# Queries and keys of a hybrid attention layer: the rotated columns of eight heads gathered into one projection unit, the plain ones into three, with the order of tasks laid out anew

## The chip, the cores and the metric

One core of one Trainium2 chip runs one launch of the whole layer. The metric is the device time of that launch in microseconds (us). The engines are TensorE (PE: matmuls; PEld: its weight loads), VectorE (DVE), ScalarE (ACT), GpSimd (POOL), and SyncE (SP), on which this kernel issues its DMAs. Each engine works through its own queue strictly in order.

## The reference, cut to what matters

The layer has 512 positions and a model width of 1024. One projection gives the queries, keys and values of two token mixers, an indexer's queries and keys, and branch gates:

```python
proj = x @ w_in            # qa ka va (12 heads), qb kb vb (12 heads), qi (8), ki (1), wi, gates
qa, ka, qi, ki, qb, kb = partial_rope(...)   # heads of 64 columns

def partial_rope(x, cos, sin):               # r = 8
    x1, x2, rest = x[..., :r], x[..., r:2 * r], x[..., 2 * r:]
    return concatenate([x1 * cos - x2 * sin, x2 * cos + x1 * sin, rest], axis=-1)
```

So of a head's 64 columns only the first 16 are rotated; the 48 others pass unchanged. Mixer A scores each query against the keys that an indexer picks (the 128 highest of up to 512, by `top_k`), mixer B attends in three dilated windows (groups of 4 heads with strides 1, 4 and 16) whose outputs are combined by their softmax denominators. Two gated branch products, an output projection, layer norm, a SwiGLU network and a second layer norm follow. All is in float32; each product is made of three matmuls on split operands (high x high, high x low, low x high).

## The kernel before, in words

**Units.** The columns of `w_in` come in units of 128 columns x 1024 rows (a `raw` tile of 128 x 1024). SP loads a unit, ACT copies its high part (`whi`, L347), DVE or POOL subtracts for the low part (`wlo`, L362), and `project()` makes 24 matmuls of 512 columns (L415 to L417) into one PSUM tile with the 128 columns of two heads on its partitions. Two such PSUM tiles exist (tag `pj`).

**Rotation.** Of the 28 units with queries and keys (28 head pairs), each goes through `rope()`: DVE shuffles the PSUM tile's partitions (L495), DVE multiplies it by a cosine table (L496), POOL multiplies the shuffled copy by a sine table (L497), and DVE adds the two (L499, or L502, which also regroups the positions by their remainder of four). The tables hold 1 and 0 for the 48 plain columns, so a full tile of 128 partitions is rotated though 32 of them change. Then `parts()` splits the result: ACT copies the high part (L508), DVE subtracts for the low part (L362).

**Stacks.** PE's scores want stacks: tiles of 128 partitions that hold a head's high part on 64 partitions and its high or low part on the other 64. `move()` assembles them by DMAs from SBUF to SBUF of 64 partitions each; SP issues 144 of them (all DMAs go through L331).

**Top-k.** `topk_steps()` finds the 128 highest of each row by 16 rounds of DVE's `MAX8` (L684) and `MATCH_REPLACE8` (L685) for each of three blocks of queries (256, 384 and 512 keys). Its rounds take turns on DVE with whatever else is queued there. Between them DVE also makes mixer B's masked scores (L768), the factors that combine its groups (L802 to L811), its output sums (L870 to L879) and the rotations.

**Order.** A string `ORDER` lists tasks: K index keys, I index heads, k/q/r/s and a/b units of mixers B and A, v the strided values, B0 to B3 mixer B's scores, X the exchange of its statistics over DRAM, M0 to M3 its mixing, W value chunks, H0 to H5 mixer A's head pairs, G gate units, T four top-k rounds. A planner (`Plan.order`) runs the listed tasks through a model of the engines with a price for each instruction, the free slots of each pool, and turns between DVE and POOL for operations marked `shared`, and emits each engine's queue in the order that it finds. The price of a DMA is `0.06 + nbytes / 361e3` us there.

Of the kernel before, what the change touches and what calls it, by code (L numbers as in the profile page):

```python
# [51 lines left out]
ORDER = ("G12 k0 r1 q0 G14 K G0 I1 r0 v I0 s0 b1 I3 G5 I2 G13 s1 r3 T s3 T a1 G2 B1 r2 k1 T q1 B0 B3 s2 B2 T T W0 T "  # L52
         "a4 X M2 G9 W1 a0 H1 b0 T M1 G7 T a3 M3 b5 M0 W2 T b2 a5 H0 b3 G8 H3 b4 G4 H5 a2 G11 G3 H2 H4 T T G1 G15 T "
         "G6 G10").split()

H = (slice(0, 64), slice(64, 128))
SWAP = list(range(8, 16)) + list(range(8)) + list(range(16, 32))
# [233 lines left out]
def layer(ctx, tc, xT, xN, pos, wp, bg, ln, cst, out):  # L291
# [38 lines left out]
    def dma(dst, dst_ap, src_ap, nbytes, reads=(), key=None, prio=None):  # L330
        P.op("SP", 0.06 + nbytes / 361e3, lambda e: nc.sync.dma_start(dst_ap(), src_ap()),  # L331
             reads, [(dst, key)], lag=DMA_LAG, prio=prio)
# [4 lines left out]
    def load_unit(lo_eng, pieces=1):  # L337

        u = unit[0]
        unit[0] += 1  # L340
        raw, hi, lo = P.buf("raw", FT, (128, 1024)), P.buf("whi", FR, (128, 1024)), P.buf("wlo", FR, (128, 1024))
        n = 1024 // pieces

        def piece(i):
            c = slice(i * n, (i + 1) * n)
            dma(raw, lambda: raw[:, c], lambda: wp[u * 128:(u + 1) * 128, c], 512 * n, key=i)
            P.op("ACT", ac(n, 1), lambda e: A.activation(hi[:, c], raw[:, c], AF.Copy), [(raw, i)], [(hi, i)])  # L347
            sub(lo_eng, n, lambda: lo[:, c], lambda: raw[:, c], lambda: hi[:, c].bitcast(FT),
                [(raw, i), (hi, i)], [(lo, i)])
# [55 lines left out]
    def next_unit(lo_eng):  # L405
        return first_units.pop(0) if first_units else load_unit(lo_eng)

    def project(w, tag="pj", t0=0):

        hi, lo, pieces, _ = w  # L410
        p = P.buf(tag)
        for ko in range(KO):
            def f(e, ko=ko):
                c = slice(ko * 128, (ko + 1) * 128)
                nc.tensor.matmul(p[:, t0:], hi[:, c], xhi[ko][:, t0:], start=ko == 0, stop=False)  # L415
                nc.tensor.matmul(p[:, t0:], hi[:, c], xlo[ko][:, t0:], start=False, stop=False)  # L416
                nc.tensor.matmul(p[:, t0:], lo[:, c], xhi[ko][:, t0:], start=False, stop=ko == KO - 1)  # L417
            k = ko * pieces // KO
            P.op("PE", 3 * mm(S - t0), f, [(hi, k), (lo, k), xhi[ko], xlo[ko]], [p])
        return p  # L420


    def rope_tables():
        n = NB * 8
        r_ = [fixed(f"rope{i}", (128, n)) for i in range(8)]
        pf, ang, c, d, hi, lo, u, r = r_
        prod = P.buf("rp", FT, (128, 2 * N_PIECE, n))
        rnd = P.buf("rp", FT, (128, 2 * N_PIECE, n))

        def v(cost, fn, reads, writes):  # L430
            P.op("DVE", cost, lambda e: fn(), reads, writes, prio=20)
# [31 lines left out]
        sn, cn = P.buf("rp", FT, (128, NB, 2, 8)), P.buf("rp", FT, (128, NB, 8))  # L463
        P.op("ACT", 0.15, lambda e: A.activation(sn[:, :, 1, :], a3(u), AF.Sin, scale=TWO_PI), [u], [(sn, 1)])
        P.op("ACT", 0.15, lambda e: A.activation(cn.tile, a3(r), AF.Sin, scale=TWO_PI), [r], [cn])
        v(small, lambda: V.tensor_scalar(sn[:, :, 0, :], sn[:, :, 1, :], -1.0, None, ALU.mult), [(sn, 1)], [(sn, 0)])
        for h in (0, 64):
            v(dv(64), lambda h=h: V.tensor_copy(wide_s[:, :, h:h + 16], sn.tile.rearrange("p b a f -> p b (a f)")),
              [sn], [(wide_s, h)])
            v(dv(64), lambda h=h: V.tensor_copy(wide_c[:, :, h:h + 16].rearrange("p b (a f) -> p b a f", a=2),  # L470
                                                bc(cn[:, :, None, :], [128, NB, 2, 8])), [cn], [(wide_c, h)])
# [14 lines left out]
    sn_rows, cn_rows = (lambda: sn[:, :, 1, :]), (lambda: cn.tile)  # L486
# [5 lines left out]
    def rope(p, regroup=False, t0=0):  # L492
# [4 lines left out]
        P.op("POOL", po(n), lambda e: G.tensor_tensor(t[:, t0:], t[:, t0:], TS[:, t0:], ALU.mult), [t, TS], [t])  # L497
# [8 lines left out]
    def parts(r, lo_tag, hi_tag="rt", t0=0):  # L506
        hi, lo = P.buf(hi_tag, FR), P.buf(lo_tag, FR)
# [4 lines left out]
    def move(dst, d, src, s, t0=0):  # L512
        dma(dst, lambda: dst[H[d], t0:].bitcast(FT), lambda: src[H[s], t0:].bitcast(FT), 256 * (S - t0), [src], d)

    def q_stacks(r, t0=0):

        hi, lo = parts(r, "rt", t0=t0)
        o = []
        for e in range(2):
            s = P.buf("qk", FR)  # L520
            move(s, e, hi, e, t0)
            move(s, 1 - e, lo, e, t0)
            o.append(s)
        return o

    def k_stacks(r):

        o = []
        for part in parts(r, "rt"):
            for e in range(2):  # L530
                s = P.buf("qk", FR)
                for x in range(2):
                    move(s, x, part, e)
                o.append(s)
        return [(o[0], o[2]), (o[1], o[3])]

    def k_blocks(r):

        o = []
        for part in parts(r, "rt"):  # L540
            for x in range(2):
                t = P.buf("qk", FR)
                P.op("POOL", 0.46, lambda e, t=t: G.memset(t.tile.bitcast(FT), 0.0), [], [t])
                for e in range(2):
                    dma(t, lambda t=t, e=e: t.tile.bitcast(FT).rearrange("p (r e m) -> p r e m", r=2, e=2)[H[e], :, e],
                        lambda part=part, x=x, e=e: part.tile.bitcast(FT).rearrange("p (r m) -> p r m", r=4)[
                            H[e], 2 * x:2 * x + 2], 65536, [part], e)
                o.append(t)
        return o[:2], o[2:]
# [113 lines left out]
    def index_heads(pr):  # L663

        qs = q_stacks(rope(project(next_unit("POOL"), t0=128), t0=128), t0=128)
# [13 lines left out]
    def topk_steps():  # L679
        for b in range(1, NB):  # L680
            n = (b + 1) * 128
            for _ in range(TOPK // 8):
                m = P.buf("z", FT, (128, 8))
                P.op("DVE", dv(n), lambda e, m=m, b=b: V.max(m.tile, acc[b].tile), [acc[b]], [m])  # L684
                P.op("DVE", dv(n), lambda e, m=m, b=b: V.match_replace(acc[b].tile, m.tile, acc[b].tile, TAKEN),  # L685
                     [acc[b], m], [acc[b]])
                yield
            P.op("DVE", dv2(n), lambda e, b=b: V.tensor_scalar(acc[b].tile, acc[b].tile, -2.0e38, NEG,
                                                               ALU.is_gt, ALU.mult), [acc[b]], [acc[b]])
# [104 lines left out]
    def b_factors(own, other, name):  # L794
# [6 lines left out]
        v = lambda fn, r, w: P.op("DVE", c, lambda e: fn(), r, w)  # L801
# [28 lines left out]
    def b_mix(i, dst):  # L830
# [48 lines left out]
        P.op("DVE", dv(512), lambda e: V.tensor_add(dst[d], x1[d], x2[d]), [x1, x2], [(dst, odd)])  # L879
# [57 lines left out]
    def q_pair(name):  # L937
        store[name] = q_stacks(rope(project(next_unit("POOL"))))

    def k_pair(name):  # L940
        store[name] = k_stacks(rope(project(next_unit("POOL"))))

# [3 lines left out]
        "q": lambda i: q_pair(f"q{i}"),  # L946
        "k": lambda i: k_pair(f"k{i}"),
        "r": lambda i: store.update({f"r{i}": parts(rope(project(next_unit("POOL")), True), "qk", "qk")}),
        "s": lambda i: store.update({f"s{i}": k_blocks(rope(project(next_unit("POOL")), True))}),
        "v": strided_values,  # L950
        "B": lambda i: b_logits(i, store[f"q{i // 2}"][i % 2], store[f"k{i // 2}"][i % 2],
                                store[f"r{i}"], store[f"s{i}"]),
# [3 lines left out]
        "a": lambda i: q_pair(f"a{i}"),  # L956
        "b": lambda i: k_pair(f"b{i}"),
        "H": lambda n: a_pair(n, store[f"VA{n // 2}"], store[f"a{n}"], store[f"b{n}"], out_tile(n)),
# [233 lines left out]
def _pack(np, inputs):  # L1192
# [76 lines left out]
```

## Time and profile before

| | |
|---|---|
| runs shown | 886.59, 888.36, 888.82 us (median 888.36) |
| profiled execution | 886.41 us, its span 884.6 us |
| busy share of PE, DVE, ACT, POOL | 96%, 59%, 41%, 19% |
| mean granted TensorE clock | 0.990 |

The span runs from the first to the last instruction; 1.8 us of the profiled execution lie around it. A busy PE is not PE at its peak: where the granted clock is below 1, the same matmuls take longer. The projections, both mixers and the top-k fill about the first 430 us; branch products, output projection and feed-forward network follow.

### The profile page before, as it was taken

What the parts mean: (1) busy time and instruction counts of PE and PEld (TensorE: products, weight loads), DVE (VectorE), ACT (ScalarE), POOL (GpSimd) and SP (SyncE); (2) the same over time, 40 slices, a digit from 0 to 9 for tenths busy, and PEclk for the clock granted to TensorE, in tenths of its full rate; (3) what the DMA queues carried; (4) which work ended last, traced back from release to release, by engine and by line L of the source; (5) the groups of instructions that cost most, each with busy time, mean ns of one, the idle gap of its engine ahead of it and who ended that gap; (6) DMA issues with size and microseconds to landing.
All of it is one profiled execution on the core that took longest, in us unless ns stands there. A gap on an engine that the chain in (4) does not pass through costs nothing.

```text
span 884.6 us, 11508 instructions
## 1 busy us (share of the span) xinstructions
PE 853.0 (96%) x4183; PEld 723.9 (82%) x4183; DVE 519.1 (59%) x1132; ACT 361.3 (41%) x769; POOL 167.8 (19%) x115
## 2 busy tenths in 40 slices
PE   8999999988889999999999999999999999999996
PEld 5888988878778888888888898888888888888885
DVE  7636467998996866868576853333333333222357
ACT  5333344345477546969644132222222222221210
POOL 3634544743332342320000100000000000000001
PEclk9999999999999999999999999999999999999999
DMA  6623362444415345321436303232233222222321
GB/s 206 190 96 114 114 183 71 129 130 121 122 49 143 90 141 151 97 96 48 156 113 231 120 16 104 95 98 97 101 101 103 98 96 95 96 96 96 119 72 72
DMA packets 41321, 98.69 MB, mean 112 GB/s; under 512 B 6960, under 2 KB 13360, under 8 KB 41264
## 3 DMA queue, kind: packets, MB, share of 16 engines
q1 hardware_dynamic: 41264, 97.95, 35.4%
q8 instruction: 33, 0.54, 0.3%
q14 instruction: 24, 0.20, 0.1%
HBM read 79.55 MB, written 2.13 MB: 92 GB/s over the span
## 4 chain that ended last, share of the span: by engine, by line
PE 75%; DVE 14%; DMA 3%; issue 2%; ACT 2%; SPq 2%; POOL 1%; DVEq 0%; POOLq 0%; ACTq 0%
PE ps L1092 9%; PE ps L1093 9%; PE ps L1094 9%; PE ps L1121 5%; PE ps L1119 5%; PE ps L1120 5%; PE ps L415 4%; PE ps L416 4%; PE ps L417 4%; PE ps L566 2%; DVE s L685 2%; DVE z L684 2%; PE ps L722 2%; PE ps L1059 2%; PE ps L1060 2%
## 5 line engine op out<-in xcount | busy, mean ns | idle before, releaser
L347 ACT ACTIVATE whi<-raw 128x1024 fp32r<-128x1024 f32 (+2 forms) x133 | 134.4, 1013 | 205.9 <-issue 83.4
L362 DVE TENSOR_TENSOR wlo<-raw,whi 128x1024 fp32r<-128x1024 f32 (+1 forms) x83 | 98.5, 1187 | 165.3 <-ACT whi L347 165.3
L362 POOL TENSOR_TENSOR wlo<-raw,whi 128x1024 fp32r<-128x1024 f32 (+2 forms) x50 | 115.3, 2310 | 152.7 <-ACT whi L347 139.2
L415 PE MATMUL ps<-s,whi 128*128 128x512 f32 (+1 forms) x352 | 141.2, 401 | 0.5 <-ACT s L391 0.5
L1092 PE MATMUL ps<-s,whi 128*128 128x512 f32 (+1 forms) x368 | 139.8, 380 | 0.0
L1093 PE MATMUL ps<-s,whi 128*128 128x512 f32 (+1 forms) x368 | 139.8, 380 | 0.0
L1094 PE MATMUL ps<-s,wlo 128*128 128x512 f32 (+1 forms) x368 | 139.8, 380 | 0.0
L416 PE MATMUL ps<-s,whi 128*128 128x512 f32 (+1 forms) x352 | 137.6, 391 | 1.8 <-DVE s L362 1.7
L417 PE MATMUL ps<-s,wlo 128*128 128x512 f32 (+1 forms) x352 | 136.8, 389 | 0.0
L1032 POOL TENSOR_TENSOR z<-z,nhalf 128x1 f32<-128x1 f32 x8 | 7.6, 955 | 479.3 <-DVE z L1031 479.3
L1094 PEld LDWEIGHTS ps<-s,wlo 128*128 128x128 f32 x368 | 69.2, 188 | 13.2
L1092 PEld LDWEIGHTS ps<-s,whi 128*128 128x128 f32 x368 | 69.2, 188 | 13.2
L1093 PEld LDWEIGHTS ps<-s,whi 128*128 128x128 f32 x368 | 69.2, 188 | 12.9
L416 PEld LDWEIGHTS ps<-s,whi 128*128 128x128 f32 x352 | 67.2, 191 | 13.8 <-DVE s L362 4.1
L417 PEld LDWEIGHTS ps<-s,wlo 128*128 128x128 f32 x352 | 66.8, 190 | 13.1
L415 PEld LDWEIGHTS ps<-s,whi 128*128 128x128 f32 x352 | 67.2, 191 | 11.7 <-ACT s L391 1.6
L362 DVE TENSOR_TENSOR s<-s,s 128x512 fp32r<-128x512 f32 (+1 forms) x74 | 52.7, 714 | 7.6 <-ACT s L508 4.2
L1119 PE MATMUL ps<-whi,s 128*128 128x512 f32 x136 | 52.9, 389 | 0.0
L1120 PE MATMUL ps<-wlo,s 128*128 128x512 f32 x136 | 52.9, 389 | 0.0
L1121 PE MATMUL ps<-whi,s 128*128 128x512 f32 x136 | 52.9, 389 | 0.0
L497 POOL TENSOR_TENSOR s<-s,tab 128x512 f32<-128x512 f32 (+1 forms) x28 | 35.5, 1268 | 78.6 <-DVE s L495 62.7
L1106 ACT ACTIVATE s<-ps 128x512 f32<-128x512 f32 x22 | 13.2, 598 | 86.8 <-PE ps L1094 86.8
(167 smaller groups left out, 1531.2 us busy)
## 6 DMA issues: line engine op xcount, KB each, us to landing
raw<-in_wp SPq DMA_DIRECT2D x136, 512.0 KB, 3.2
s<-s SPq DMA_DIRECT2D x96, 128.0 KB, 2.3
s<-in_xT SPq DMA_DIRECT2D x8, 256.0 KB, 4.7
s<-s SPq DMA_DIRECT2D x32, 64.0 KB, 2.0
s<-in_ln SPq DMA_DIRECT2D x8, 256.0 KB, 4.7
s<-in_xN SPq DMA_DIRECT2D x8, 256.0 KB, 5.3
out<-s SPq DMA_DIRECT2D x7, 256.0 KB, 2.1
s<-s SPq DMA_DIRECT2D x16, 96.0 KB, 2.5
```

What stands on the lines that cost most here:

```text
L347: P.op("ACT", ac(n, 1), lambda e: A.activation(hi[:, c], raw[:, c], AF.Copy), [(raw, i)], [(hi, i)])
L362: P.op(eng, cost, lambda e: ENG[e].tensor_tensor(dst(), a(), b(), ALU.subtract), reads, writes, shared=True)
L415: nc.tensor.matmul(p[:, t0:], hi[:, c], xhi[ko][:, t0:], start=ko == 0, stop=False)
L416: nc.tensor.matmul(p[:, t0:], hi[:, c], xlo[ko][:, t0:], start=False, stop=False)
L417: nc.tensor.matmul(p[:, t0:], lo[:, c], xhi[ko][:, t0:], start=False, stop=ko == KO - 1)
L497: P.op("POOL", po(n), lambda e: G.tensor_tensor(t[:, t0:], t[:, t0:], TS[:, t0:], ALU.mult), [t, TS], [t])
L1092: nc.tensor.matmul(p[:, c], hi[:, k], x1hi[ko][:, c], start=ko == 0, stop=False)
L1093: nc.tensor.matmul(p[:, c], hi[:, k], x1lo[ko][:, c], start=False, stop=False)
L1094: nc.tensor.matmul(p[:, c], lo[:, k], x1hi[ko][:, c], start=False, stop=ko == KO - 1)
L1119: nc.tensor.matmul(sums[:, :cols], hs[k][0][:, t], hi(), start=k == first, stop=False)
L1120: nc.tensor.matmul(sums[:, :cols], hs[k][0][:, t], lo(), start=False, stop=False)
L1121: nc.tensor.matmul(sums[:, :cols], hs[k][1][:, t], hi(), start=False, stop=k == last)
```

## The change

The 28 units stay 28, but are cut otherwise. For each eight heads (seven groups: the indexer's, three of mixer A, three of mixer B) unit 0 holds the 8 x 16 rotated columns and units 1 to 3 hold the 8 x 48 plain ones. Only unit 0 is rotated (7 instead of 28), and its second multiplication is made by DVE, not POOL. The plain units are split straight from PSUM: ACT copies the high part, DVE subtracts. A head now lies in two or three tiles, so its stacks are put together from pieces of 16, 32 or 48 rows, and SP issues 348 such DMAs instead of 144. POOL's low parts of the weights are made in halves of 512 columns, of which the first can be used earlier; the tables are made by one broadcast copy each; the planner's price of a DMA is at least 0.44, some more DVE operations are marked `shared`, and two top-k prices are a little higher. `ORDER` is new.

```diff
-ORDER = ("G12 k0 r1 q0 G14 K G0 I1 r0 v I0 s0 b1 I3 G5 I2 G13 s1 r3 T s3 T a1 G2 B1 r2 k1 T q1 B0 B3 s2 B2 T T W0 T "
+ORDER = ("G10 i0 G12 G6 i1 d0 i2 e0 W0 d1 i3 K G7 G13 e1 I1 e2 e4 I2 e3 I0 d2 a8 I3 B1 G15 T T T e5 B0 G2 e6 a0 d3 "
...
-        P.op("POOL", po(n), lambda e: G.tensor_tensor(t[:, t0:], t[:, t0:], TS[:, t0:], ALU.mult), [t, TS], [t])
+        P.op("DVE", dv(n), lambda e: V.tensor_mul(t[:, t0:], t[:, t0:], TS[:, t0:]), [t, TS], [t], shared=True)
...
+    def plain_parts(p, regroup, t0):
+        hi, lo = P.buf("rt", FR), P.buf("rt", FR)
+        to = (lambda t: reg(t.tile)) if regroup else lambda t: t[:, t0:]
+        src = (lambda: nat(p.tile)) if regroup else lambda: p[:, t0:]
+        P.op("ACT", ac(S - t0), lambda e: A.activation(to(hi), src(), AF.Copy), [p], [hi])
+        P.op("DVE", dv(S - t0), lambda e: V.tensor_tensor(to(lo), src(), to(hi).bitcast(FT), ALU.subtract),
+             [p, hi], [lo])
+        return hi, lo
...
+    def move(dst, d, src, s, n, t0=0):
+        dma(dst, lambda: dst[d:d + n, t0:].bitcast(FT), lambda: src[s:s + n, t0:].bitcast(FT), 4 * n * (S - t0),
+            [src], d)
...
+    def sides(name, j, puts, regroup=False, t0=0):
+
+        p = project(next_unit("POOL"), t0=t0)
+        if j == 0:
+            turned[name] = rotated_parts(p, regroup, t0)
+            return
+        parts = plain_parts(p, regroup, t0)
+        for s, put in enumerate(puts):
+            for unit_, row, n, first in plain_rows(s):
+                if unit_ == j - 1:
+                    if first == 0:
+                        put(turned[name], ROT * s, ROT, 0)
+                    put(parts, row, n, ROT + first)
...
-        "q": lambda i: q_pair(f"q{i}"),
-        "k": lambda i: k_pair(f"k{i}"),
...
+        "i": lambda j: sides("i", j, [put_q(f"i{h}", 128) for h in range(8)], t0=128),
+        "a": lambda n: sides(f"a{n // 4}", n % 4, qk_sides("a", n // 4 * 4)),
+        "d": lambda j: sides("d", j, qk_sides("d", 0)),
+        "e": lambda n: sides(f"e{n // 4}", n % 4, rs_sides(n // 4), True),
...
+    def side_unit(j, firsts):
+
+        rot = [w_in[:, c:c + ROT] for c in firsts]
+        rest = [w_in[:, c + ROT:c + 64] for c in firsts]
+        tile_unit(np.concatenate(rot, 1) if j == 0 else np.concatenate(rest, 1)[:, (j - 1) * 128:j * 128])
```

What this does to the queues shows best in three places. The first is DVE between two rounds of the first top-k block. Before, the sum of one rotation (L502) and the first rows of the next (L495 shuffle, L496 cosine) stand there (`s_121` is the block's scores):

```order
L502 TENSOR_TENSOR s_1525<-s_1476,s_1468 128x128x4
L495 STREAM_SHUFFLE s_1532<-ps_1456 128x512
L496 TENSOR_TENSOR s_1534<-ps_1456,tab_89 128x512
L685 MATCH_REPLACE s_121<-z_1518,s_121 128x256
L684 MAX z_1544<-s_121 128x8
L685 MATCH_REPLACE s_121<-z_1544,s_121 128x256
```

In the changed kernel the rows at that place are mostly plain splits (L536) and mixer B's scores (L834, before L768); the block's scores are `s_113`:

```order
L751 MATCH_REPLACE s_113<-z_1667,s_113 128x256
L750 MAX z_1690<-s_113 128x8
L834 ISA s_1703,z_91<-ps_1685,cs 128x128
L834 ISA z_91 128x1
L751 MATCH_REPLACE s_113<-z_1690,s_113 128x256
L536 TENSOR_TENSOR s_1712<-ps_1579,s_1692 128x128x4
L750 MAX z_1718<-s_113 128x8
L834 ISA s_1703,z_91<-ps_1694,cs 128x256
```

A unit that took three DVE rows before its split now takes none; between the first and the last `MAX` stand 246 DVE rows before and 220 after, with nine rotations before and two after.

The second place is SP's queue. Before, a unit's stacks are eight moves of 64 rows behind one weight load, here a unit of group s (`64x2x128`) behind the split of an index head:

```order
L331 DMA raw_1252<-in_wp 128x1024
L331 DMA raw_1292<-in_wp 128x1024
L331 DMA s_1327<-s_1319 64x384
L331 DMA s_1331<-s_1319 64x384
L331 DMA s_1327<-s_1325 64x384
L331 DMA s_1331<-s_1325 64x384
L331 DMA raw_1357<-in_wp 128x1024
L331 DMA s_1403<-s_1440 64x2x128 x2
L331 DMA s_1407<-s_1440 64x2x128 x2
```

In the changed kernel, before mixer B's first scores, moves of 16, 32 and 48 rows from the rotated tile (such as `s_531`) and a plain one (`s_1428`, `s_1437`) stand behind each other:

```order
L346 DMA raw_1430<-in_wp 128x1024
L346 DMA s_618<-s_1428 16x512
L346 DMA s_618<-s_1437 16x512
L346 DMA s_1411<-s_1428 48x512 x2
L346 DMA s_1421<-s_1437 48x512 x2
L346 DMA raw_1463<-in_wp 128x1024
L346 DMA s_1517<-s_531 16x512 x2
L346 DMA s_1527<-s_549 16x512 x2
L346 DMA s_1517<-s_1428 48x512 x2
L346 DMA s_1527<-s_1437 48x512 x2
L346 DMA s_1565<-s_531 16x512
```

Weight loads (`raw`) now stand behind more moves than before, and a stack is complete only when the last of its four to six pieces has landed.

The third place is PE's queue between mixer B's scores and its mixing, whose transposes are L722 (after: L788). Before, two units (L415 to L417, 48 rows) and 30 rows of a value chunk (L579 to L581) lie between the last scores (L558) and the first transpose, which these rows reach:

```order
L581 MATMUL ps_2325<-wlo_2294,s_277 128x256
L579 MATMUL ps_2378<-whi_2221,s_151 128x256
L580 MATMUL ps_2378<-whi_2221,s_160 128x256
L581 MATMUL ps_2378<-wlo_2237,s_151 128x256
L579 MATMUL ps_2378<-whi_2221,s_164 128x256
L580 MATMUL ps_2378<-whi_2221,s_175 128x256
L581 MATMUL ps_2378<-wlo_2237,s_164 128x256
L722 MATMUL ps_2390<-cs,s_2150 128x128
```

After, the strided values (`v`, L678 to L680, 96 rows of 512 columns) lie there; these are their end:

```order
L678 MATMUL ps_2312<-whi_2361,s_264 128x512
L679 MATMUL ps_2312<-whi_2361,s_271 128x512
L680 MATMUL ps_2312<-wlo_2372,s_264 128x512
L678 MATMUL ps_2320<-whi_2361,s_264 128x512
L679 MATMUL ps_2320<-whi_2361,s_271 128x512
L680 MATMUL ps_2320<-wlo_2372,s_264 128x512
L788 MATMUL ps_2533<-cs,s_2104 128x128
```

PE has 4030 such rows before and after, and from the last gate unit on its queue is the same. The `v` rows stood earlier in the queue before.

## Rows read from the trace of the kernel before

**Rows 1.** Busy time by stretch (a:b, length, PE, PEld, DVE, ACT, POOL, clock, DMA, GB/s).

```profile
0.00:50.00 50.00, 45.88 (x210) 37.03 (x211) 31.39 (x64) 22.02 (x39) 20.09 (x24) 1.00 0.61 186
50.00:143.70 93.70, 89.16 (x430) 80.88 (x429) 51.11 (x77) 36.17 (x61) 44.63 (x27) 1.00 0.42 126
143.70:260.10 116.40, 105.87 (x588) 92.77 (x587) 111.66 (x303) 59.67 (x148) 50.58 (x33) 0.96 0.37 108
260.10:380.00 119.90, 115.98 (x663) 99.43 (x662) 92.16 (x293) 79.78 (x229) 42.48 (x22) 0.99 0.42 115
380.00:500.00 120.00, 119.21 (x572) 99.29 (x571) 88.45 (x201) 70.05 (x166) 4.38 (x3) 1.00 0.42 140
...
800.00:885.00 85.00, 76.90 (x354) 64.11 (x352) 39.03 (x64) 13.08 (x17) 3.69 (x4) 0.97 0.26 88
```

**Rows 2.** What PE waited for: total us, times, longest.

```profile
PE ps L566 <- DMA s<-s: 4.6, 3, 3.2
PE ps L722 <- ACT s L827: 3.9, 1, 3.9
...
PE ps L558 <- DVE z L768: 2.9, 1, 2.9
```

**Rows 3.** Instructions of the top-k's MAX8: min/median/max ns, first and last start.

```profile
L684 DVE MAX8 z<-s x48: 401/556/698, 143.7 to 259.4; 128x8 f32<-128x256 f32 x16, 128x8 f32<-128x384 f32 x16, 128x8 f32<-128x512 f32 x16
```

**Rows 4.** DVE's groups by shape, 143.7 to 260.1 us.

```profile
L502 DVE TENSOR_TENSOR s<-s,s 128x512 f32<-128x512 f32 x5 | 8.2, 1646 | 0.0
...
L495 DVE STREAM_SHUFFLE s<-ps 128x512 f32<-128x512 f32 x9 | 6.8, 752 | 0.0
...
L496 DVE TENSOR_TENSOR s<-ps,tab 128x512 f32<-128x512 f32 x9 | 6.1, 675 | 0.0
L362 DVE TENSOR_TENSOR s<-s,s 128x512 fp32r<-128x512 f32 x9 | 6.0, 680 | 0.0
L499 DVE TENSOR_TENSOR s<-s,s 128x512 f32<-128x512 f32 x4 | 4.8, 1202 | 0.0
...
L877 DVE TENSOR_TENSOR s<-ps,s 64x256 f32<-64x256 f32 x6 | 2.4, 416 | 0.1
...
L826 DVE TENSOR_SCALAR s<-s,f 128x256 f32<-128x256 f32 x2 | 0.7, 345 | 0.0
```

**Rows 5.** Timeline of PE, part of 188 to 200 us (start, length, idle before in brackets).

```profile
190.86 0.39 PE L416 MATMUL ps<-s,whi 128*128 128x512 f32 x1
191.09 0.39 PE L417 MATMUL ps<-s,wlo 128*128 128x512 f32 x1
194.38 0.89 PE L558 MATMUL ps<-s,s 128*128 128x256 f32 x3 [2.91 <-DVE z L768]
195.07 0.63 PE L415 MATMUL ps<-s,whi 128*128 128x512 f32 x1
195.50 0.63 PE L416 MATMUL ps<-s,whi 128*128 128x512 f32 x1
```

**Rows 6.** SP's issues (L331): min/median/max ns, first and last start; then one burst.

```profile
L331 SPq DMA_DIRECT2D raw<-in_wp x146: 327/328/709, 0.7 to 843.0; - x146
L331 SPq DMA_DIRECT2D s<-s x144: 461/589/1522, 27.9 to 381.9; - x144
...
175.28 7.84 SPq L331 DMA_DIRECT2D s<-s  x12
```

**Rows 7.** DMAs by kind: count, KB each, median us from issue to landing.

```profile
s<-s SPq DMA_DIRECT2D x96, 128.0 KB, 2.3
...
s<-s SPq DMA_DIRECT2D x32, 64.0 KB, 2.0
```

**Rows 8.** Splits straight from PSUM: one DVE subtraction (L654), ACT's copies (L1106).

```profile
L654 DVE TENSOR_TENSOR s<-ps,s x1: 693/693/693, 58.6 to 58.6; 128x512 fp32r<-128x512 f32 x1
...
L1106 ACT ACTIVATE s<-ps 128x512 f32<-128x512 f32 x22 | 13.2, 598 | 86.8 <-PE ps L1094 86.8
```

**Rows 9.** POOL's multiplications, 143.7 to 260.1 us.

```profile
L497 POOL TENSOR_TENSOR s<-s,tab 128x512 f32<-128x512 f32 x9 | 11.6, 1291 | 29.3 <-DVE s L495 29.3
```

More of the change, by code (lines that the diff above doesn't have):

```diff
@@ L430, in v @@
         def v(cost, fn, reads, writes):
-            P.op("DVE", cost, lambda e: fn(), reads, writes, prio=20)
+            P.op("DVE", cost, lambda e: fn(), reads, writes, prio=20, shared=True)
         small = dv(n)
@@ L510, in parts @@
         return hi, lo
[L512 to L531, printed above, removed]
-                for x in range(2):
-                    move(s, x, part, e)
-                o.append(s)
-        return [(o[0], o[2]), (o[1], o[3])]
@@ L537, in k_blocks @@
[L537 to L549, printed above, removed]
+    def plain_parts(p, regroup, t0):
+        hi, lo = P.buf("rt", FR), P.buf("rt", FR)
+        to = (lambda t: reg(t.tile)) if regroup else lambda t: t[:, t0:]
[4 more added lines that the diff above has]
+        return hi, lo
@@ new lines, in layer, with stack, put_q, put @@
+    stacks = {}
+    def stack(name):
+        if name not in stacks:
+            stacks[name] = P.buf("qk", FR)
+        return stacks[name]
+    def move(dst, d, src, s, n, t0=0):
+        dma(dst, lambda: dst[d:d + n, t0:].bitcast(FT), lambda: src[s:s + n, t0:].bitcast(FT), 4 * n * (S - t0),
+            [src], d)
+    def put_q(name, t0=0):
+        def put(parts, s, n, d):
+            for x in range(2):
+                move(stack(name), 64 * x + d, parts[x], s, n, t0)
+        return put
@@ new lines, in put_k, with put, put_r, put_s @@
+    def put_k(name):
+        def put(parts, s, n, d):
+            for x in range(2):
+                for y in range(2):
+                    move(stack(f"{name}.{x}"), 64 * y + d, parts[x], s, n)
+        return put
+    def put_r(name, e):
+        def put(parts, s, n, d):
+            for x in range(2):
+                move(stack(f"{name}.{x}"), 64 * e + d, parts[x], s, n)
+        return put
+    def put_s(name, e):
+        def put(parts, s, n, d):
+            for i, part in enumerate(parts):
+                for x in range(2):
+                    new = f"{name}.{i}{x}" not in stacks
+                    t = stack(f"{name}.{i}{x}")
+                    if new:
+                        P.op("POOL", 0.46, lambda _, t=t: G.memset(t.tile.bitcast(FT), 0.0), [], [t])
+                    o = 64 * e + d
+                    dma(t, lambda t=t: t.tile.bitcast(FT).rearrange("p (r e m) -> p r e m", r=2, e=2)[o:o + n, :, e],
+                        lambda part=part, x=x: part.tile.bitcast(FT).rearrange("p (r m) -> p r m", r=4)[
+                            s:s + n, 2 * x:2 * x + 2], 1024 * n, [part], o)
+        return put
@@ new lines, in qk_sides, with rs_sides @@
+    def qk_sides(name, h):
+        q, k = (lambda x: put_q(f"{name}q{h + x}")), (lambda x: put_k(f"{name}k{h + x}"))
+        return [q(0), k(0), q(1), k(1), k(2), q(2), k(3), q(3)]
+    def rs_sides(g):
+        r, s = (lambda x, e: put_r(f"r{2 * g + x}", e)), (lambda x, e: put_s(f"s{2 * g + x}", e))
+        return [r(0, 0), s(0, 0), r(0, 1), s(0, 1), s(1, 0), r(1, 0), s(1, 1), r(1, 1)]
+    two = lambda name: [stacks[f"{name}.{x}"] for x in range(2)]
+    four = lambda name: [[stacks[f"{name}.{i}{x}"] for x in range(2)] for i in range(2)]
@@ L663, in index_heads @@
     def index_heads(pr):
-        qs = q_stacks(rope(project(next_unit("POOL"), t0=128), t0=128), t0=128)
+        qs = [stacks[f"i{2 * pr + x}"] for x in range(2)]
         kh, kl, wi = idx["kh"], idx["kl"], idx["wi"]
```

96 lines of the change are left out of this document (49 added, 47 removed).

## The prediction, made before the changed kernel had run

> **What bounds the kernel now.** The stretches come first, to see where PE loses time. In [rows 1] the reader subtracts PE's busy time from each length and adds what the granted clock takes of it, (1 − clock) x length. From 0 to 50 us that is 4.1, from 50 to 143.7 us 4.5, from 143.7 to 260.1 us 10.5 + 4.7 = 15.2, from 260.1 to 380 us 3.9 + 1.2 = 5.1, from 380 to 500 us 0.8. From 500 us PE has no gaps until the last stretch, which loses 8.1 idle + 2.5 and which the change does not touch. So PE bounds the kernel almost everywhere, and about half of the 30 us that it loses before 500 us lies in 116 us. That stretch is the top-k: its first MAX8 starts at 143.7 and its last at 259.4 [rows 3]. There DVE is busy 111.7 of 116.4 us [rows 1], and so DVE is the bound, not PE: the PE work done in it is 105.9 − 4.7 = 101 us at full clock.
>
> The waits say the same. PE's longest single ones are for DVE's scores (L768, 2.9), for ACT's scaling by the factors that DVE computes (L827, 3.9) and for DMAs of stacks (4.6 in three waits, one of 3.2) [rows 2]. After the 2.91 us wait at 194.4 the matmuls, which started 0.23 us apart before it, start 0.43 us apart [rows 5]: a wait also costs some us of lower clock, which is the 4.7 in the sum above.
>
> What shares DVE with the top-k is in [rows 4]. The nine rotations of the stretch take 6.8 (shuffle) + 6.1 (cosine) + 8.2 + 4.8 (sums) + 6.0 (split) = 31.9 us, by far the largest thing that is not top-k.
>
> **The change part by part.** PE has the same rows before and after, so only its losses can move.
>
> *Top-k stretch, DVE.* By the order, two rotations stand between the first and the last MAX8 instead of nine. Removed: 31.9 us. Added: two rotations, each 0.75 + 0.68 [rows 4], a multiplication by the sine table and a sum. The trace has no such multiplication on DVE with both inputs in SBUF; the nearest rows of that shape are the split at 0.68 and the sums at 1.20 and 1.65 [rows 4], so each of the two rows is 0.68 to 1.65; I take 1.0, since fewer of them meet a busy POOL (below). That makes 2 x 3.4 = 6.9. Also three rotated splits at 0.68 (2.0), five plain splits at 0.69 [rows 8] (3.5), three half weight units at 0.7 for one whole one, estimated at twice 0.68 (+0.7), nine more scalings (L826, 0.345 each, 3.1) [rows 4]. Moved out: six of the mixing's additions (2.4) [rows 4] and two of its 512-column rows (by the 0.68 of that shape 1.4, one stays), and six index accumulations (L675, 256 to 512 columns; 0.6 each by the 0.68 of 512, 3.6); with a few scores fewer I take −8. Together −31.9 + 16.2 − 8 = −23.7. Neighbouring rows of DVE overlap: the groups of the stretch add up to 128 us by their own durations, while DVE is busy 111.7, so 0.87 of it counts: −20.7, and DVE's busy time becomes 91 us. With the 4.7 us of waits that it has now, the stretch lasts about 95 us.
>
> *Top-k stretch, PE.* By the order the tiles that DVE reads before its first and before its last MAX8 have 193,920 matmul columns between them on PE: at 0.23 us per 512 [rows 5] 87 us, some 88 with the transposes, which run slower per column. So the loss there falls from 15.2 to about 95 − 88 = 7. **Gain: 8.** Bounds: if POOL's and DVE's collisions vanish with the rotations the sums fall away, and the loss is 3; if DVE's waits double, it is 12.
>
> *Exchange.* The 3.9 us wait for the scaled factors is part of the 15.2. Before, 48 matmuls of 512 and 30 of 256 columns cover the exchange, 14.5 us at the pace of [rows 5]; now the 96 of `v` and the unit around them do, 22 us. I count this inside the stretch, as one of the ways by which 7 is reached.
>
> *Index heads and first scores.* Their stacks came late in three waits, 4.6 us in all; the one of 3.2 lies in the top-k stretch, so 1.4 lie outside [rows 2]. In the new order the index stacks are finished tens of us of PE work ahead of their use. **Gain: 1.5.**
>
> *PSUM.* A projected tile was free after shuffle and cosine (1.4 us), now for plain units after ACT's copy and DVE's subtraction, 0.60 + 0.69 = 1.3 [rows 8]. Nothing.
>
> *Mixer A.* The six head pairs stand closer together behind the mixing, in some 100 us of PE work where they had 150. The stretch from 260.1 to 380 us has DVE at 92 of 120 us and ACT at 80 [rows 1]; moved closer, both rise by some 10% but stay under the length. I charge **1** of new waits, between 0 and 5.
>
> *SP.* 204 more moves. One takes SP 0.59 us, 0.46 at the least [rows 6], and in a burst 7.84/12 = 0.65 [rows 6]: 94 to 133 us more of SP, all beside PE. In the densest part, the 50 us of PE work before mixer B's scores, the order has 82 moves and 7 weight loads: 82 x 0.59 + 7 x 0.33 = 51 us [rows 6]. SP is full there. What it costs depends on slack: the tightest stacks of the new order are wanted about 10 us of PE work after the unit that makes their last piece, where those of before were wanted after 6. By issues at 0.62 no stack comes late; at 0.65 the slack is down to about 1 us. I charge nothing and leave this as the largest risk.
>
> The Trainium skill, "DMA: Bandwidth & Descriptors", "Rules for kernel authors", speaks against this part: many small transfers are to be made into one large, since under 64 KB one pays mostly overhead. The trace agrees: 64 KB land in 2.0 us and 128 KB in 2.3 [rows 7]. By the rule cutting moves into 32 to 96 KB pieces saves nothing on each and multiplies the fixed cost, which is the direction of rival 1.
>
> *POOL.* It loses the multiplications, 11.6 us in the stretch [rows 9]. DVE's sums of two SBUF tiles took 1.20 and 1.65 us where the split of the same shape took 0.68 [rows 4]: 5 x 0.97 + 4 x 0.52 = 6.9 us of stretching, counted in the 31.9. The Trainium skill, "SBUF — State Buffer", "Who interferes with whom", has it that a DVE instruction with two SBUF inputs and a GpSimd instruction that reads SBUF exclude each other. By that rule the new multiplication and sum can each wait for half a weight unit on POOL, which is inside the 0.68 to 1.65 above.
>
> **The sum.** Against the profiled execution, 886.4: −8 −1.5 +1 = 877.9; the exchange's longer cover and the smaller clock loss after fewer waits are in the 8. I forecast **877.5 us**. The profiled execution lies 0.2% under the median of the runs shown (888.36), so a median of the changed kernel may lie 1 to 2 us above its profile; 0.3% of the time, 2.7 us, is what a measurement of this kernel can tell from no change.
>
> **The rivals.**
>
> 1. *SP and its moves become the bound (slower).* If a move costs 0.70 instead of 0.62 in the dense part, 82 of them put SP 6.6 us further behind, and the pieces also hold the tiles that they read: DVE's next split waits for a free tile, with top-k rounds queued behind it in order. Several DVE rows of the new order ahead of and in the top-k wait on DMAs. Six waits of 3 us, as long as the longest stack wait of [rows 2], are 18 us on the engine that bounds the stretch: 877.5 + 18 = 895. It decides from about 11 us of such waits. For it: SP at 51 of 50 us, and weight loads queued behind the moves. Against it: 10 us of slack, and raw loads of 0.33 us that catch up.
>
> 2. *DVE's saving is given back (no change).* If the rounds of MAX8 and MATCH_REPLACE8 wait on scores and splits in their new places, DVE's busy time falls but its idle time grows from 4.7 to some 13 us, and the stretch keeps its loss: 886. For it: PE and DVE are now within 3 us of each other in the stretch (88 and 91), so small waits of either hurt both. Against: the plain split needs one hop, PE to ACT to DVE, where a rotation needed DVE, POOL, DVE, ACT, DVE.
>
> 3. *Mixer A gets the waits instead.* With 5 us there: 882.
>
> 4. *More gain.* The stretch loses 3 and the exchange nothing: 886.4 − 12 − 1.5 = 873, and with a third of the 4.5 + 5.1 lost around the stretch 870; 866 with both.
>
> That the change does not do what it says is excluded by the order: 7 shuffles instead of 28, and 204 more moves.
>
> **Chances.** The forecast with its own range, 870 to 883.5: 0.52. More gain, below 870: 0.12. Mixer A's waits, 882 to 884: 0.04. No change, within 2.7 us of 886.4: 0.13. Slower: 0.19. So faster 0.68, same 0.13, slower 0.19. The range that leaves out 2 in 10 goes from 866 to 892: the lower end is rival 4 with all its parts, the upper one lies two thirds of the way to rival 1's 895.
>
> **What would show it.** Right: between the first and last MAX8 some 95 us instead of 116; DVE busy about 91 of them; no wait of about 4 us at the mixing's first transposes; a clock of 0.98 or more there; two rotations instead of nine; sums nearer 0.7 than 1.6. SP: 348 moves at 0.55 to 0.62, PE's waits on DMAs no more than 4.6 us. Wrong: PE or DVE waiting on DMAs for more than 10 us in all, or weight loads that land after PE wants them (waits of L430 to L432), or DVE's busy time in the stretch over 100 us, or over 8 us of PE's losses in the mixer A stretch.

## The result, and the profile after

The changed kernel takes 873.31 us (median of 4 runs, 870.81 to 875.07) against 887.48 for the kernel before: a ratio of 0.984, 95% interval 0.980 to 0.987. The forecast was 877.5 with a range of 866 to 892, so the change was faster as forecast, by 14 us where 9 were expected. The profiled execution took 875.07 us with a span of 873.3, 11.3 less than the span before.

The busy time by stretch, cut as in [rows 1] at the top-k's first and last MAX8 and then by time:

```profile
0.00:50.00 50.00, 45.86 (x201) 36.76 (x202) 25.86 (x61) 22.70 (x38) 17.32 (x22) 1.00 0.52 168
50.00:148.70 98.70, 97.75 (x530) 86.34 (x529) 45.44 (x75) 39.75 (x67) 46.98 (x43) 1.00 0.48 142
148.70:247.10 98.40, 91.80 (x433) 79.20 (x433) 87.95 (x273) 51.03 (x130) 34.09 (x29) 0.98 0.44 127
247.10:370.00 122.90, 120.40 (x728) 105.42 (x727) 80.56 (x268) 76.35 (x222) 32.10 (x24) 0.99 0.44 128
370.00:500.00 130.00, 129.11 (x623) 107.14 (x623) 96.63 (x225) 72.83 (x180) 9.11 (x7) 1.00 0.36 122
...
800.00:873.30 73.30, 65.86 (x305) 54.97 (x303) 36.59 (x62) 10.96 (x15) 3.95 (x4) 0.98 0.25 87
```

Length less busy plus (1 − clock) x length gives PE's losses as in the prediction: 4.1, then 1.0 (4.5 before), 6.6 + 2.0 = 8.6 (15.2 before), 2.5 + 1.2 = 3.7 (5.1 before), 0.9 (0.8). So 6.6 us came from the top-k stretch, 3.5 from the one ahead of it and 1.4 from mixer A's; with differences of some tenths elsewhere that is about the span's 11.3.

PE's waits (total us, times, longest) have changed their nature; those of [rows 2] are gone or under 1 us, and the longest is now for a weight unit's high part:

```profile
PE ps L430 <- ACT whi L362: 3.6, 2, 3.3
PE ps L432 <- POOL wlo L380: 1.9, 3, 0.6
PE ps L820 <- DVE s L809: 1.7, 3, 1.1
```

The top-k lasts from 148.7 to 246.4 us, 98 us instead of 116 [rows 3]:

```profile
L750 DVE MAX8 z<-s x48: 418/559/695, 148.7 to 246.4; 128x8 f32<-128x256 f32 x16, 128x8 f32<-128x384 f32 x16, 128x8 f32<-128x512 f32 x16
```

DVE's groups by shape in that stretch answer to [rows 4]: two rotations, plain splits, and two sums (L517) at 683 ns, where the means before were 1202 (L499) and 1646 (L502, which also regroups):

```profile
L536 DVE TENSOR_TENSOR s<-ps,s 128x512 fp32r<-128x512 f32 x5 | 4.6, 924 | 8.4 <-ACT s L535 8.4
...
L892 DVE TENSOR_SCALAR s<-s,f 128x256 f32<-128x256 f32 x11 | 3.4, 350 | 0.0
...
L513 DVE STREAM_SHUFFLE s<-ps 128x512 f32<-128x512 f32 x2 | 1.5, 736 | 0.0
...
L515 DVE TENSOR_TENSOR s<-s,tab 128x512 f32<-128x512 f32 x2 | 1.4, 686 | 0.0
L517 DVE TENSOR_TENSOR s<-s,s 128x512 f32<-128x512 f32 x2 | 1.4, 683 | 0.0
```

The first of these rows also shows what is new: DVE sits idle 8.4 us in front of plain splits, in two waits, for ACT's copies of them (L535). Why these are late shows in the timelines from 142 to 196 us. SP (start, length, count) issues up to 24 moves in a row, and 16 moves in 10.33 us ahead of one weight load:

```profile
142.25 16.33 SPq L346 DMA_DIRECT2D s<-s  x24
...
173.93 10.33 SPq L346 DMA_DIRECT2D s<-s  x16
184.35 0.53 SPq L346 DMA_DIRECT2D raw<-in_wp  x1
184.93 1.14 SPq L346 DMA_DIRECT2D s<-s  x2
186.18 0.52 SPq L346 DMA_DIRECT2D raw<-in_wp  x1
186.81 7.93 SPq L346 DMA_DIRECT2D s<-s  x12
```

ACT stands 4.32 us for that load, with the copy L535 queued behind it:

```profile
188.23 1.06 ACT L362 ACTIVATE whi<-raw 128x1024 fp32r<-128x1024 f32 x1 [4.32 <-DMA raw<-in_wp]
189.19 0.58 ACT L535 ACTIVATE s<-ps 128x512 fp32r<-128x512 f32 x1
```

DVE stands for the copy with MAX8 queued behind the split, and PE for the high part; after it PE's matmuls start 0.42 to 0.43 us apart instead of 0.23, as in [rows 5] (granted clock 0.77 from 189 to 192 us, 1.00 from 185 to 189). The first line is the other long wait of a plain split; it goes the same way, for ACT had stood 5.95 us for a weight load just before:

```profile
174.92 1.08 DVE L536 TENSOR_TENSOR s<-ps,s 128x512 fp32r<-128x512 f32 x1 [4.72 <-ACT s L535]
...
189.80 0.69 DVE L536 TENSOR_TENSOR s<-ps,s 128x512 fp32r<-128x512 f32 x1 [3.70 <-ACT s L535]
190.41 0.55 DVE L750 MAX8 z<-s 128x8 f32<-128x384 f32 x1
```

```profile
185.65 0.39 PE L432 MATMUL ps<-s,wlo 128*128 128x512 f32 x1
189.34 0.50 PE L430 MATMUL ps<-s,whi 128*128 128x512 f32 x1 [3.30 <-ACT whi L362]
...
191.29 0.63 PE L430 MATMUL ps<-s,whi 128*128 128x512 f32 x1
191.71 0.63 PE L431 MATMUL ps<-s,whi 128*128 128x512 f32 x1
```

So the gain is there, and a part of it is handed back by the queue of rival 1. The experiments ask how much each part is worth.

### The profile page after: what moved, and what is told of

Same layout as the page of the kernel before. It is cut to its first block, busy times and chain, and to the rows that moved or that the text cites. A ratio compares the mean times of both kernels' runs of the same rounds, so it can differ in the third digit from the quotient of the medians.

```text
span 873.3 us, 11770 instructions
## 1 busy us (share of the span) xinstructions
PE 850.8 (97%) x4183; PEld 720.3 (82%) x4183; DVE 474.2 (54%) x1078; ACT 354.7 (41%) x755; POOL 144.5 (17%) x129
## 4 chain that ended last, share of the span: by engine, by line
PE 77%; DVE 6%; ACT 5%; DMA 5%; SPq 4%; issue 1%; POOL 1%; DVEq 0%; ACTq 0%; POOLq 0%
PE ps L1151 9%; PE ps L1150 9%; PE ps L1152 9%; PE ps L430 6%; PE ps L432 6%; PE ps L431 6%; DMA raw<-in_wp 5%; PE ps L1177 5%; PE ps L1178 5%; PE ps L1179 5%; SPq L346 4%; PE ps L632 2%; PE ps L788 2%; PE ps L1117 1%; PE ps L1118 1%
## 5 line engine op out<-in xcount | busy, mean ns | idle before, releaser
L380 DVE TENSOR_TENSOR wlo<-raw,whi 128x1024 fp32r<-128x1024 f32 (+2 forms) x93 | 100.7, 1085 | 166.9 <-ACT whi L362 166.7
L380 POOL TENSOR_TENSOR wlo<-raw,whi 128x512 fp32r<-128x512 f32 x94 | 125.7, 1358 | 249.4 <-ACT whi L362 215.5
L430 PE MATMUL ps<-s,whi 128*128 128x512 f32 (+1 forms) x352 | 142.3, 404 | 3.8 <-ACT whi L362 3.6
L430 PEld LDWEIGHTS ps<-s,whi 128*128 128x128 f32 x352 | 67.3, 191 | 15.0 <-ACT whi L362 4.4
L809 DVE TENSOR_TENSOR s<-ps,s 128x128 fp32r<-128x128 f32 (+1 forms) x144 | 39.0, 317 | 12.2 <-ACT s L807 11.8
L1165 DVE TENSOR_TENSOR s<-s,ps 128x512 f32<-128x512 f32 x22 | 15.1, 688 | 55.4 <-PE ps L1152 55.3
```

Of the source, the lines that this page charges most:

```text
L380: P.op(eng, cost, lambda e: ENG[e].tensor_tensor(dst(), a(), b(), ALU.subtract), reads, writes, shared=True)
L809: subs.append((dv(m), lambda e, src=src, dst=dst, hi=hi, ho=ho, lo=lo, lo_o=lo_o: V.tensor_tensor(dst(lo, lo_o), src(), dst(hi, ho).bitcas ...
```

## The experiments

All were timed in rounds with the kernel before, whose median was 886.9 to 887.3 us in them. Times below are medians of 4 runs unless a count is given. e1, e2 and e11 keep the changed kernel's order in every queue and only add, drop or shrink rows; in all other runs the planner lays the queues out anew, so some of their difference can be the layout's (e5 below shows how much that can be).

**More DVE time in the plain splits** (label e1).

```diff
-        P.op("DVE", dv(S - t0), lambda e: V.tensor_tensor(to(lo), src(), to(hi).bitcast(FT), ALU.subtract),
-             [p, hi], [lo])
+        def f(e):
+            for _ in range(4):
+                V.tensor_tensor(to(lo), src(), to(hi).bitcast(FT), ALU.subtract)
+        P.op("DVE", dv(S - t0), f, [p, hi], [lo])
```

> The changed kernel with the subtraction of each of the 21 plain units issued four times over (three repeats of 0.69 us, 2.1 us per unit), all queues otherwise the same and the result unchanged. Theory (the gain is the rotations' time taken off DVE in the top-k stretch): about five of the units lie in that stretch, 10 us more on DVE; the stretch already has some 8 us of DVE idle time behind a late split, so part of it hides: slower by 4 to 10 us than the changed kernel, 877 to 883. Rival (the gain is the new order, DVE has slack everywhere): within 2 us of the changed kernel.

Measured: 896.98 us, ratio 1.010 (1.008 to 1.013) to the kernel before, 24 us slower than the changed one. That is far more than either theory had: 44 us of DVE time (21 x 2.1) cost 24. The stretches (first and last MAX8 at 155.2 and 262.6) show that not only the top-k pays:

```profile
50.00:155.20 105.20, 99.43 (x524) 86.94 (x524) 60.70 (x96) 39.04 (x67) 46.19 (x43) 0.97 0.43 134
155.20:263.30 108.10, 96.20 (x430) 81.16 (x430) 101.01 (x287) 49.97 (x127) 34.09 (x29) 0.95 0.38 115
263.30:390.00 126.70, 119.53 (x714) 103.40 (x714) 92.39 (x272) 72.94 (x208) 31.02 (x24) 0.99 0.42 124
```

PE loses 8.9, 17.3 and 8.4 us in them instead of 1.0, 8.6 and 3.7. So the top-k stretch alone pays 8.7 us more, within the 4 to 10 that the theory gave it; what it missed are the units outside that stretch, whose DVE time it took to be free. Each split also has its moves behind it on SP, so a later split probably makes SP's queue later too; that link was not measured by itself.

**The rotations alone** (label e9). The kernel before, with its own units, moves, prices and order, but 21 of 28 units take the plain path.

```diff
     def rope(p, regroup=False, t0=0):
+        turn[0] += 1
+        if turn[0] % 4 != 1:
+            return p, regroup
...
+        if isinstance(r, tuple):
+            return plain_parts(*r, lo_tag, hi_tag, t0)
```

> The kernel before with its own order string, units, moves and prices, but 21 of its 28 units split straight from PSUM without rotation (three of four in the order of the tasks; their first 16 columns of each head stay unrotated, so the output is another). Theory (DVE's rotation rows in the top-k stretch are what is paid for): two to three of nine rotations remain in that stretch, 8 to 13 us faster than before, 875 to 879. Rival (the gain is the new order of tasks): within 3 us of before.

Measured: 876.80 us, ratio 0.987 (0.986 to 0.989), 10 us faster than before, inside what the theory said and away from the rival's. Leaving the rotations out is worth about 10 us without any of the rest.

**The order alone** (labels e3 and e10). First one task of the kernel before moved:

```diff
-G0 I1 r0 v I0 s0
+G0 I1 r0 I0 s0
...
-a4 X M2 G9
+a4 X v M2 G9
```

> The kernel before with one task moved: the strided values v behind the exchange X instead of behind r0, as in the changed order. Theory (rotations first, the exchange's cover a part inside the stretch): the wait of 3.9 us at the mixing's first transposes goes, but v's cover is missing earlier; between 3 us faster and 3 us slower than before. Rival (the new order's later v is the main gain): 6 to 12 us faster than before.

Measured: 888.18 us (10 runs), ratio 1.0005 (0.9995 to 1.0015): nothing. Of PE's waits the one of 3.9 us at the first transposes is only renamed, and two others are longer than in [rows 2]:

```profile
PE ps L566 <- DMA s<-s: 6.2, 2, 4.2
PE ps L558 <- DVE z L768: 4.6, 1, 4.6
PE ps L722 <- DVE s L592: 4.1, 1, 4.1
```

Then the kernel of e9 with a whole order after the changed kernel's:

```diff
+ORDER = ("G10 k0 G12 G6 q0 r1 s1 W0 K G7 G13 I1 I2 r0 I0 s0 I3 B1 G15 T T T B0 G2 k1 q1 s2 r2 T T T B2 s3 T r3 "
+         "G9 T B3 a1 X v T M2 b1 G8 T M1 a2 M3 T b2 W2 T M0 a0 b0 T H1 G11 a3 W1 H2 b3 H0 a4 H3 b4 G3 G14 H4 a5 b5 "
+         "H5 G5 G4 G0 G1")
```

> The kernel before with 21 of 28 units split plainly (as in the run that gave 876.8) and the tasks of its units put in an order after the changed kernel's: index heads, scores, v behind the exchange, mixer A's pairs last; 144 moves, the output another. If the new order is worth the 16 us that lie between that run and the one with 160 moves in the new order (860.9): 861 to 868. If it is the cut of the units that makes the order work (no stack waits for its own unit's rotation): 873 to 880.

Measured: 865.70 us, ratio 0.974 (0.972 to 0.977): 11 us faster than e9. The order as a whole is worth as much as the rotations, once these are gone; moving v alone in the kernel before is worth nothing. Two rotations stand in the top-k stretch of both e9 and e10, so the difference is not theirs. The top-k stretches, first e9's and then e10's:

```profile
137.80:220.30 82.50, 74.54 (x399) 64.77 (x399) 79.23 (x231) 38.88 (x94) 30.77 (x21) 0.96 0.38 110
134.80:222.30 87.50, 84.06 (x400) 74.30 (x398) 85.92 (x267) 51.25 (x128) 37.83 (x23) 0.97 0.39 115
```

By the same sum as above PE loses 11.3 us in e9's and 6.1 in e10's, where the kernel before lost 15.2. Without the rotations the stretch is 34 us shorter, but PE's work in it shrinks almost as much, and only about 4 of e9's 10 us are gained there. The new order puts more PE work beside DVE's top-k and brings another 5.

**The moves** (labels e2 and e11). In e2 the moves are taken from the emitted queue only: PE, DVE, ACT and POOL keep the changed kernel's rows. Each half stack gets one move of 64 rows from its last piece's tile.

```diff
-        dma(dst, lambda: dst[d:d + n, t0:].bitcast(FT), lambda: src[s:s + n, t0:].bitcast(FT), 4 * n * (S - t0),
-            [src], d)
+        last, o, y = d % 64 + n == 64, d // 64 * 64, min(s, 64)
+        dma(dst, lambda: dst[o:o + 64, t0:].bitcast(FT), lambda: src[y:y + 64, t0:].bitcast(FT), 4 * n * (S - t0),
+            [src], d, on=last)
```

> The changed kernel with one move of 64 rows in place of the two or three pieces of each half stack: 160 moves instead of 348, the queues of all other engines the same; the stacks then hold other columns than the reference's, so the output is another. Theory (SP is full from 142 to 195 us, weight loads queued behind 16 to 24 moves come late, ACT's and then DVE's queue stand): DVE's 8.4 us of waits for the plain splits and PE's 3.6 us for whi go, 4 to 7 us faster than the changed kernel, 866 to 869. Rival (SP is hidden, those waits come from elsewhere): within 2 us of the changed kernel.

Measured: 860.90 us, ratio 0.970 (0.968 to 0.971): 12.4 us faster than the changed kernel, twice what was expected. The top-k stretch of e2 and the one behind it, and SP's timeline there, against those above:

```profile
146.60:238.00 91.40, 90.15 (x438) 79.26 (x437) 87.84 (x273) 50.87 (x130) 34.11 (x29) 1.00 0.42 125
238.00:370.00 132.00, 131.75 (x809) 116.25 (x807) 89.81 (x309) 86.12 (x255) 36.41 (x27) 1.00 0.45 130
```

```profile
180.92 4.96 SPq L346 DMA_DIRECT2D s<-s  x8
185.98 1.04 SPq L346 DMA_DIRECT2D raw<-in_wp  x2
192.21 6.13 SPq L346 DMA_DIRECT2D s<-s  x8
```

PE loses 1.3 us in the stretch instead of 8.6 and 0.3 behind it instead of 3.7; DVE has the same 87.8 us of work. SP has gaps between its bursts. In e11 all 348 moves are issued again, but every piece except the last of a half stack carries one row:

```diff
+        m = 64 if last else 1
+        dma(dst, lambda: dst[o:o + m, t0:].bitcast(FT), lambda: src[y:y + m, t0:].bitcast(FT), 4 * n * (S - t0),
+            [src], d)
```

> The changed kernel with all 348 moves issued, but of each half stack's pieces only the last carries rows (64 of them) and the others one row each; the bytes are about those of the run with 160 moves, the output is another. If the changed kernel's cost of 12 us is SP's time to issue, nothing is won: 870 to 875. If it is the transfers themselves (bytes, landing, DMA engines), it comes near the run with 160 moves: 860 to 864.

Measured: 875.35 us, ratio 0.986 (0.984 to 0.988): all that e2 had won is lost again to 188 moves of 1 to 2 KB. SP's issues (min/median/max ns) take as long, and the burst at the same place as above too:

```profile
L346 SPq DMA_DIRECT2D s<-s x348: 467/587/1480, 29.1 to 363.8; - x174
```

```profile
175.70 10.31 SPq L346 DMA_DIRECT2D s<-s  x16
186.11 0.53 SPq L346 DMA_DIRECT2D raw<-in_wp  x1
```

ACT's waits for weight loads (total us, times, longest) go the same way; the lines are the kernel before, the changed one, e2 and e11:

```profile
ACT whi L347 <- DMA raw<-in_wp: 27.3, 13, 8.9
ACT whi L362 <- DMA raw<-in_wp: 76.8, 29, 9.5
ACT whi L362 <- DMA raw<-in_wp: 30.0, 14, 7.7
ACT whi L362 <- DMA raw<-in_wp: 76.1, 31, 9.2
```

So it is the number of issues on SP, not the bytes. That the landing of the many pieces is not it either is less directly shown: PE's waits in the changed kernel list none for a stack's DMA, and with two queues (below) the 96 KB moves land later, in 3.0 instead of 2.3 us, and the kernel is faster all the same.

**Two smaller parts of the change** (labels e7 and e8), each undone by itself in the changed kernel.

```diff
-        P.op("DVE", dv(n), lambda e: V.tensor_mul(t[:, t0:], t[:, t0:], TS[:, t0:]), [t, TS], [t], shared=True)
+        P.op("POOL", po(n), lambda e: G.tensor_tensor(t[:, t0:], t[:, t0:], TS[:, t0:], ALU.mult), [t, TS], [t])
```

> The changed kernel with the second multiplication of its seven rotations back on POOL. Theory (seven rows of 0.69 us hardly count): within 2 us of the changed kernel. Rival (taking POOL out of the rotation's chain is a main part of the gain): 4 us or more slower.

```diff
-            m = n if lo_eng == "DVE" else min(n, 512)
+            m = n
```

> The changed kernel with POOL's low parts of the weights made whole again (1024 columns at once). Theory: within 3 us of the changed kernel. Rival (halves let PE start units 1.3 us earlier and shorten the collisions of DVE and POOL, a main part of the gain): 5 us or more slower.

Measured: 871.55 us (ratio 0.983, 0.980 to 0.985) and 871.42 us (0.983, 0.980 to 0.985). Their intervals and the changed kernel's overlap: neither part's effect is clear of the noise, and the 4 or 5 us of the rivals are excluded.

**The planner's price and a second queue** (labels e5, e6, e12, e13). First only the price:

```diff
-        P.op("SP", max(0.44, 0.06 + nbytes / 361e3), lambda e: nc.sync.dma_start(dst_ap(), src_ap()),
+        P.op("SP", 0.62 if prio is None and dst.tag in moved else max(0.44, 0.06 + nbytes / 361e3),
+             lambda e: nc.sync.dma_start(dst_ap(), src_ap()),
```

> The changed kernel with the planner's price of a stack move at 0.62 us, as measured, instead of 0.44; the moves stay 348 on SP, all queues are laid out anew. If the loss is that the planner thinks SP idle when it is full, it now places DVE's and ACT's waits better: 866 to 872. If SP's time itself is the bound, the queue stays full: within 3 us of 873.

Measured: 880.16 us, ratio 0.993 (0.991 to 0.994): 7 us slower than the changed kernel, which neither side had expected. PE now waits 7.4 us in four times for the high parts of weights. With the task order fixed, another layout by the planner alone moves the time by 7 us, as much as some parts of the change; the differences of e9 and e10, of 10 and 11 us, are larger, but each can be off by some us for this reason. Why this layout is worse was not looked into. Then the moves on SP or ACT:

```diff
+        two = dst.tag is P.tags["qk"]
+        P.op(("SP", "ACT") if two else "SP", (0.62, 0.62) if two else max(0.44, 0.06 + nbytes / 361e3),
+             lambda e: (nc.scalar if e == "ACT" else nc.sync).dma_start(dst_ap(), src_ap()),
```

> The changed kernel with each stack move free to be issued by SP or by ACT, whichever the planner finds idle first, priced at 0.62 us on both: 188 moves on SP, 143 on ACT, the order laid out anew by the same planner. If SP's full queue is what costs the changed kernel 12 us (as the run with fewer moves has it), most of it comes back: 860 to 867, unless ACT's own queue (45 of 50 us busy at most) takes the waits over. Rival (it was not SP's issue time but the number of transfers or the landing of their pieces): within 3 us of the changed kernel's 873.

> The changed kernel with each stack move on SP or ACT, whichever the planner finds idle first, priced at 0.44 us on both. The same with 0.62 us gave 868.0; the price of 0.62 alone on SP laid out a queue that was 7 us slower than with 0.44. If that price misleads the planner there too: 860 to 865. If what is left is ACT's own time for the moves: 866 to 870.

> As the run with two queues at 0.44 us, at 0.52 us: between 860 and 870; tells how far the planner's layout by itself moves the time, when only a price changes by 0.08 us.

Measured: 867.96 us at 0.62 (ratio 0.978, 0.976 to 0.980), 866.60 at 0.44 (0.975, 0.973 to 0.978), 865.19 at 0.52 (0.974, 0.972 to 0.976). All three beat both kernels; the last is the fastest found with the layer's own output, 8 us under the changed kernel. Its issues by SP and ACT:

```profile
L349 SPq DMA_DIRECT2D s<-s x206: 507/582/1977, 29.2 to 348.3; - x103
L349 ACTq DMA_DIRECT2D s<-s x142: 511/600/1935, 29.2 to 347.4; - x142
```

Of the 12.4 us that SP cost, 5.4 to 8.1 came back, a part of it perhaps by the new layouts. The three prices differ by 3 us, with intervals that touch, so no price is shown to be the best.

## Why the prediction was right, point by point

**The bound.** Right: the top-k stretch was DVE's, and taking rotations off DVE shortened it from 116 to 98 us (95 forecast), DVE's busy time there from 111.7 to 88 (91 forecast). PE's loss in it fell by 6.6 us; the forecast was 8. e9 shows that the rotations are a cause without the rest of the change: 10 us. But the prediction put its 8 us down to DVE's rows and took PE's work in the stretch as the new order has it; e9 and e10 part the two: of 9 us less loss in that stretch about 4 come with the rotations and 5 with the order. Of the prediction's own signs those of being right came (DVE busy 88 us, two rotations, sums at 0.68, a clock of 0.98, no wait of 4 us at the first transposes), and one of being wrong came beside them: PE waited 3.6 us at L430 for high parts of weights.

**The sums.** The new multiplication and the sums took 0.69 and 0.68 us in the stretch, the lower end of the 0.68 to 1.65 given. The reading behind that range was off. Of the nine sums in the stretch before, six took 0.67 to 0.68 (L499) or 1.07 to 1.09 us (L502, whose regrouping sum takes 1.09 to 1.10 in the changed kernel too); the three others took 3.29, 2.79 and 1.71, and each began while POOL made a low part of the weights, the six while it made none. So the stretching was about 5 us, not 6.9, and it met POOL's weight units, not its multiplications: with these back on POOL (e7) the two sums in the stretch take 0.68 again. The collisions have not gone; a sum of the changed kernel ahead of the top-k (last two lines) meets one as a sum before did (first two), only for a shorter time:

```profile
148.53 2.53 POOL L362 TENSOR_TENSOR wlo<-raw,whi 128x1024 fp32r<-128x1024 f32 x1
148.72 3.29 DVE L502 TENSOR_TENSOR s<-s,s 128x512 f32<-128x512 f32 x1
...
142.19 2.73 POOL L380 TENSOR_TENSOR wlo<-raw,whi 128x512 fp32r<-128x512 f32 x2 [3.96 <-DMA s<-s]
143.70 1.77 DVE L517 TENSOR_TENSOR s<-s,s 128x512 f32<-128x512 f32 x1
```

That 1.77 also lies above the prediction's 1.65. A small miss the other way: the five plain splits took 4.6 us, not 3.5, since three of them regroup (1.07 to 1.10 each). e7 and e8 show that POOL's share is not where the gain is.

**SP.** This step failed: "I charge nothing and leave this as the largest risk." The moves cost 12.4 us (e2), all by their number on SP, not their bytes (e11). The working had SP at 51 of 50 us in the dense part and trusted 10 us of slack of the stacks. The stacks were indeed not late: PE's waits list none for the DMA of a stack. The step priced the stacks' slack only. Of the weight loads in the same queue rival 1 said that they catch up at 0.33 us each; they did not, with up to 16 us of moves ahead of them, and ACT's waits for them rose from 27.3 to 76.8 us. The path was load, ACT's high part, ACT's copy behind it in order, DVE's split, MAX8 behind it in order. Rival 1 named the queue and the top-k behind DVE's waits, but its link, a split that waits for a tile held by moves, is not the one that the timelines show (DVE's waits list no DMA); and it came together with a larger gain, not instead of it.

**The rest of the order.** Under-sized. The prediction gave 1.5 us to the stretch ahead of the top-k, which gained 3.5, and charged 1 us to mixer A, where 1.4 were gained, in spite of SP. The runs lay the parts out, from before to after: rotations −10 (e9), order −11 (e10), the new units with about as few moves as before −5 (from e10's 865.7 to e2's 860.9, two orders that are alike but not the same, and with the smaller parts of the change in the latter), 188 more moves +12 (e2 to the changed kernel). So that the forecast's size came out near is luck: a gain largely not seen, up to 16 us for order and units, and a cost of 12 not charged nearly cancelled. The exchange's longer cover, which was counted as a part of the gain, is not shown: v moved alone brought nothing (e3).

**Mixer A and PSUM.** Mixer A was rightly costed at little; the loss there in the changed kernel is mostly SP's too, since e2 has 0.3 us of it. PSUM, put at nothing, was not tested by itself.

What stays open is which part of the new order carries the 11 us, how much of the single terms is the planner's layout, and why the planner's layout at a price of 0.62 is 7 us worse.

## What to carry to other kernels

When a change multiplies small DMAs, count the issue time on the queue, and then ask not only whether what they carry is late, but what else stands behind them in that queue and in the in-order queues of its consumers: here weight loads, then ACT, DVE and PE. If only the issuing engine is full, a second queue can give a part of it back, here 5 to 8 of 12 us. When a stage is bound by one engine, ask also how much work of the others the order puts beside it: about 4 us of the gain in the top-k stretch came with less DVE time and 5 with the order. And a forecast that comes out near should still be taken apart: runs that undo one part each showed two large terms of opposite sign in this one.

## What the runs showed of the hardware that was not expected

A move from SBUF to SBUF takes its queue 0.58 to 0.60 us to issue, whether it has 64 rows or one (median 587 ns for 348 moves of which 188 have one row, 592 for 160 of 64 rows), and on ACT as on SP (600 and 582), where a weight load of 512 KB takes 328 ns [rows 6]. With both queues at work the 96 KB moves land in 3.0 us instead of 2.3. The Trainium skill, "DMA: Bandwidth & Descriptors", "Issuing engines are not separate DMA queues", says that initiating DMAs on several engines saves only the sequencer's time, usually small relative to the DMA itself. The first half agrees: the moves themselves did not land sooner. The second does not fit this case: that time is a quarter or more of the DMA's 2.0 to 2.3 us [rows 7], and 142 of the 348 moves on ACT made the kernel 8 us faster, with the queues laid out anew.
